# Where the moving operand lies against the weights: other offsets inside three buffers

## The chip, the core and the metric

The kernel runs on one core of a Trainium2 chip. The metric is the device time of one execution in microseconds (us), lower is better. Before the change three runs gave a median of 2787.92 us (2786.68 to 2790.01).

Names used below: PE is TensorE (matmuls), PEld its weight loads, DVE is VectorE, ACT ScalarE, POOL GpSimd, SP SyncE. SBUF is the on-chip memory of 128 partitions from which the engines read, PSUM the memory into which matmuls accumulate.

## The reference

Two layers of a decoder trunk on 256 tokens of width 2048, in float32. Each layer is a mixer, a gated feed-forward with a causal convolution, and an additive embedding:

```python
for layer in range(DEPTH):
    mix = mixer_hgrn2_gla(x, ...) if layer % 2 == 0 else mixer_rwkv7_gdn(x, ...)
    x = layer_norm(ALPHA * x + mix, ln_mix_w[layer], ln_mix_b[layer])
    x = layer_norm(ALPHA * x + conv_ffn(x, ffn_w_up[layer], ffn_conv[layer], ffn_w_down[layer]), ...)
    x = x + jax.nn.sigmoid(x @ ple_w_gate[layer]) * (p[layer] @ ple_w_proj[layer])

def conv_ffn(x, w_up, conv_w, w_down):
    u = causal_dwconv(x @ w_up, conv_w)
    gate, val = jnp.split(u, 2, axis=-1)
    return (jax.nn.silu(gate) * val) @ w_down
```

`w_up` is 2048 x 11264, `w_down` 5632 x 2048. Each mixer has a large input projection (2048 to some 7200 or 7700 columns), recurrences over the 256 tokens, and an output projection of 2048 x 2048. The time goes into these dense products.

## The kernel before

**Data.** The state is kept transposed, with features on the partitions: 16 blocks (k) of 128 features by 256 tokens. Every dense operand is kept as two float32r halves, high and low, so that a product is made of three: weight high x state high, weight high x state low, weight low x state high. float32r is a 4-byte type that the PE multiplies in one pass; `split` (L256) makes the two halves of the weights: ACT casts `wr` to `wh` (L260), DVE subtracts to get `wl` (L261). `hilo` does the same for the state.

**The buffers of the change.** `operand` (L217) makes the buffers of the state: `bufA` and `bufB` with 16 blocks each, and, inside the feed-forward, `ht` with 6 blocks for the part of the hidden layer that does not fit into `bufA`. One block takes `XS` = 576 words of 4 bytes in a partition, that is 2304 bytes or 9 x 256. In it, from word `AOFF`, `BOFF` or `HOFF` on, stand the high half (256 tokens and two columns for layer-norm weights, 258 words) and behind it the low half, so the low half starts 1032 bytes, or 8 modulo 256, after the high half.

**Where things lie.** In the program that is built, `bufA` and `bufB` begin at byte 8320 and 45184 of a partition, both 128 modulo 256; `ht`, `wh` and `wl` begin at 160 modulo 256 in every one of their buffers, and the 128 columns of one block of weights take 512 bytes. So all blocks of all weights start at 160 modulo 256. With the offsets of before the high halves start at 128 + 96 = 224 (`bufA`, `bufB`) and 160 + 64 = 224 (`ht`): 64 bytes after the weights, modulo 256. The low halves are 72 bytes after them. The tile `plt` of the embedding projection has no offset; it starts at 224 in both halves. The allocation is the same before and after.

**Loops.** All matmuls go through `mm` (L269, L270). Each has its own load of a 128 x 128 block of weights. `acc2` (L281) is the common form: for each k one matmul of weight high with both halves of the state at once, 512 columns, and one of weight low with the high half, 256 columns. `acc` (L272) uses three of 256 columns, for which `dense_raw` (before a layer norm has ended) adds the two columns, 258. `dense_tok` and `start_tok` give token-major results: there the state block is the stationary operand, and 512 columns of weights move. Feed-forward: up-projections read `bufB` (the first ten read `bufA`, 258 columns), down-projections read `bufA` and `ht`. The second mixer's input projection reads `bufA` in the form `acc`, with the recurrences' small matmuls between them, in an order that `drive` writes out.

**Order.** Each engine runs its program in order. SP issues the weights' DMAs three tiles ahead (`RB`), ACT and DVE split them into three buffers (`WB`), PE consumes them, and results leave PSUM through ACT and DVE.

Of the kernel before, what the change touches and what calls it, by code (L numbers as in the profile page):

```python
# [25 lines left out]
ALPHA = 4.0 ** 0.25  # L26
EDEC = math.exp(-0.5)
XS = 576
AOFF = 24
BOFF = 24  # L30
HOFF = 16
RS = 1024.0
KB = 4
SL = 2
# [162 lines left out]
class Trunk:  # L197
    def __init__(self, ctx, tc, a, out):
# [7 lines left out]
        c = self.const  # L206
        self.Ax = self.operand(c, KT, "bufA", AOFF)
        self.Bx = self.operand(c, KT, "bufB", BOFF)
        self.A, self.B = self.Ax[:, :, :, :S], self.Bx[:, :, :, :S]
# [531 lines left out]
    def ffn(self, l, X, Xx, U, Ux):  # L741
        up, dn = self.a[f"up{l}"], self.a[f"dn{l}"]
        Ht = self.operand(self.ev, 2 * DH - KT, "ht", HOFF)[:, :, :, :S]
        H = [U[:, j] if j < KT else Ht[:, j - KT] for j in range(2 * DH)]
# [677 lines left out]
```

## Time and profile before

| | before |
|---|---|
| median of three runs | 2787.92 us |
| profiled execution | 2788.15 us |
| its span, first to last instruction | 2786.4 us |
| PE busy | 2749.1 us, 99% |
| weight loads (beside PE) | 2488.9 us, 89% |
| DVE busy | 2068.9 us, 74% |
| ACT busy | 1606.1 us, 58% |
| DMA, bytes read from HBM | 478.32 MB |
| granted TensorE clock, mean | 0.997 |

The span is what lies between the first and the last instruction of the profiled execution; 1.75 us lie around it. A busy share counts a matmul from its start to its modelled end. Matmuls overlap in a pipeline (a 256-column matmul lasts some 280 ns by its record), so what a matmul costs is read from the distance between one start and the next. Weight loads have a row of their own, PEld, and run beside the matmuls.

### The profile page before, as it was taken

To read this page: it belongs to the slowest core of one execution; us is meant where nothing else is said; L and a number is where in the kernel's file an instruction comes from. 1 tells how busy PE (TensorE), PEld (TensorE's weight loads), DVE (VectorE), ACT (ScalarE), POOL (GpSimd) and SP (SyncE) were. 2 spreads that over 40 slices of the span, in tenths; PEclk is the share of its full clock that TensorE was granted. 3 is DMA by queue.
4 is the path that set the end of the run, shared out by engine and by line. 5 is a ranking of instruction groups with operands and counts; after the bars stand their busy time and mean duration, and the time that the engine had idled before them with its cause. 6 is when DMAs were issued, how large, how long until landed. Compare 5 with 4: busy or idle time off the path is not lost.

```text
span 2786.4 us, 48101 instructions
## 1 busy us (share of the span) xinstructions
PE 2749.1 (99%) x18433; PEld 2488.9 (89%) x18433; DVE 2068.9 (74%) x3899; ACT 1606.1 (58%) x2698; POOL 62.8 (2%) x99
## 2 busy tenths in 40 slices
PE   9999999999999999999999999999999999999999
PEld 7888889988888888899999899899988888888898
DVE  5775778877667776787579789778977666777787
ACT  5664556755445555556566676745855445555565
POOL 0000000000000000000011111000000000000000
PEclk9999999999999999999999999999999999999999
DMA  7555555666666666656444333345566666665665
GB/s 238 161 164 155 170 181 177 190 191 188 178 190 202 188 189 179 185 184 213 157 131 118 107 118 122 102 147 178 184 189 190 179 189 199 190 188 177 187 190 175
DMA packets 147943, 483.57 MB, mean 174 GB/s; under 512 B 16672, under 2 KB 19888, under 8 KB 147712
## 3 DMA queue, kind: packets, MB, share of 16 engines
q1 hardware_dynamic: 145968, 475.98, 56.6%
q0 software_dynamic: 1280, 3.94, 0.5%
q8 instruction: 145, 2.38, 0.4%
q14 instruction: 86, 0.70, 0.1%
q10 hardware_dynamic: 464, 0.57, 0.1%
HBM read 478.32 MB, written 2.11 MB: 172 GB/s over the span
## 4 chain that ended last, share of the span: by engine, by line
PE 91%; DVE 4%; ACT 3%; DMA 1%; issue 1%; SPq 0%; ACTq 0%; DVEq 0%
PE pd L270 76%; PE pm L270 14%; DVE wl L261 1%; ACT wh L260 1%; DMA wr<-pg 1%; ACT L350 0%; DMA wr<-ewv 0%; DVE z L353 0%; PE pm L541 0%; DVE rdo L353 0%; DVE gG L458 0%; ACT gE L350 0%; DMA wr<-owo 0%; ACT L1130 0%; ACT ron L350 0%
## 5 line engine op out<-in xcount | busy, mean ns | idle before, releaser
L261 DVE TENSOR_TENSOR wl<-wr,wh 128x1024 fp32r<-128x1024 f32 (+3 forms) x983 | 1112.7, 1132 | 433.4 <-ACT wh L260 430.0
L260 ACT CAST wh<-wr 128x1024 fp32r<-128x1024 f32 (+3 forms) x983 | 959.0, 976 | 701.0 <-PE pd L270 494.2
L270 PE MATMUL pd<-bufB,wh 128*128 128x512 f32 (+1 forms) x3264 | 1042.9, 376 | 0.9 <-DVE z L359 0.9
L270 PE MATMUL pd<-bufA,wh 128*128 128x256 f32 (+1 forms) x3744 | 1008.4, 341 | 1.3 <-ACT wh L260 1.3
L270 PE MATMUL pd<-bufB,wl 128*128 128x256 f32 x3008 | 815.5, 281 | 0.0
L270 PE MATMUL pd<-bufA,wl 128*128 128x256 f32 x2768 | 763.8, 283 | 1.4 <-DVE wl L261 1.2
L270 PEld LDWEIGHTS pd<-bufA,wh 128*128 128x128 f32 x3744 | 643.7, 191 | 69.7 <-ACT wh L260 1.6
L270 PEld LDWEIGHTS pd<-bufB,wh 128*128 128x128 f32 x3264 | 590.6, 190 | 104.0 <-ACT wh L260 1.1
L270 PEld LDWEIGHTS pd<-bufB,wl 128*128 128x128 f32 x3008 | 565.7, 188 | 13.3
L270 PEld LDWEIGHTS pd<-bufA,wl 128*128 128x128 f32 x2768 | 522.8, 189 | 12.2 <-DVE wl L261 3.3
L300 ACT COPY dsum<-pd 128x256 f32<-128x256 f32 x204 | 75.9, 372 | 254.5 <-PE pd L270 254.4
L353 DVE TENSOR_TENSOR dsum<-dsum,pd 128x256 f32<-128x256 f32 x204 | 85.8, 421 | 128.1 <-ACT dsum L300 127.9
L359 DVE SCALAR_TENSOR_TENSOR cu<-dsum,col,cu 128x255 f32<-128x255 f32 (+1 forms) x312 | 150.3, 482 | 5.6
L270 PE MATMUL pm<-bufB,wh 128*128 128x258 f32 x768 | 139.6, 284 | 1.5 <-DVE bufB L359 1.5
L270 PE MATMUL pd<-ht,wh 128*128 128x512 f32 x384 | 136.0, 392 | 0.0
L270 PEld LDWEIGHTS pm<-bufB,wh 128*128 128x128 f32 x768 | 118.4, 189 | 2.2 <-DVE bufB L359 1.9
L270 PE MATMUL pm<-bufA,wh 128*128 128x258 f32 x640 | 116.0, 284 | 0.0
L270 PE MATMUL pm<-bufB,wl 128*128 128x258 f32 x384 | 108.7, 283 | 0.8 <-DVE wl L261 0.8
L270 PE MATMUL pd<-ht,wl 128*128 128x256 f32 x384 | 107.3, 279 | 0.0
L270 PEld LDWEIGHTS pm<-bufA,wh 128*128 128x128 f32 x640 | 98.6, 189 | 0.3 <-DVE bufA L359 0.2
L270 PE MATMUL pm<-bufA,wl 128*128 128x258 f32 x320 | 90.3, 282 | 0.0
L270 PEld LDWEIGHTS pd<-ht,wh 128*128 128x128 f32 x384 | 73.1, 190 | 15.9
(366 smaller groups left out, 2648.0 us busy)
## 6 DMA issues: line engine op xcount, KB each, us to landing
wr<-up SPq DMA_DIRECT2D x352, 512.0 KB, 4.2
wr<-ow SPq DMA_DIRECT2D x120, 512.0 KB, 3.9
wr<-dn SPq DMA_DIRECT2D x128, 384.0 KB, 3.4
wr<-ew SPq DMA_DIRECT2D x82, 512.0 KB, 4.1
wr<-dn SPq DMA_DIRECT2D x128, 320.0 KB, 3.1
wr<-pg SPq DMA_DIRECT2D x64, 512.0 KB, 4.5
wr<-ewo SPq DMA_DIRECT2D x32, 512.0 KB, 4.4
wr<-ewv SPq DMA_DIRECT2D x30, 512.0 KB, 3.9
```

The lines of the kernel that those rows point to most:

```text
L260: self.nc.scalar.copy(wh, w)
L261: self.nc.vector.tensor_sub(wl, w, wh.bitcast(F32))
L270: return self.nc.tensor.matmul(o, lhsT=l, rhs=r, start=start, stop=stop)
L300: self.nc.scalar.copy(u, o[:, S:])
L353: self.nc.vector.tensor_tensor(o, a, b, op)
L359: self.nc.vector.scalar_tensor_tensor(o, a, s, b, op0, op1)
```

## The change

Three constants change, and with them where in its block of 2304 bytes the state stands: `bufA` from byte 96 to 48, `bufB` from 96 to 128, `ht` from 64 to 208. The high halves then start at 176, 0 and 112 modulo 256, which is 16, 96 and 208 bytes after the weights, and the low halves at 24, 104 and 216. In the token-major products, in which the weights move and `bufA` is stationary, the moving operand starts 240 (232 for the low half) bytes after the stationary one instead of 192 (184).

```diff
@@ -26,9 +26,9 @@
 ALPHA = 4.0 ** 0.25
 EDEC = math.exp(-0.5)
 XS = 576
-AOFF = 24
-BOFF = 24
-HOFF = 16
+AOFF = 12
+BOFF = 32
+HOFF = 52
 RS = 1024.0
 KB = 4
 SL = 2
```

Instructions, their order on each engine and all tile addresses are the same.

## Rows read from the trace of the kernel before

**Rows 1.** The page's part 1: busy time, share of the span, count of instructions.

```profile
PE 2749.1 (99%) x18433; PEld 2488.9 (89%) x18433; DVE 2068.9 (74%) x3899; ACT 1606.1 (58%) x2698; POOL 62.8 (2%) x99
```

**Rows 2.** The page's part 4: the chain that ended last, by engine.

```profile
PE 91%; DVE 4%; ACT 3%; DMA 1%; issue 1%; SPq 0%; ACTq 0%; DVEq 0%
```

**Rows 3.** PE's waits: waiting line, awaited line, us in total, times, longest.

```profile
PE pd L270 <- ACT wh L260: 7.6, 3, 5.8
```

**Rows 4.** The view of the cores: span, mean granted TensorE clock.

```profile
core 0: 2786.4 us, clock 0.997
```

**Rows 5.** Timeline, PE, dense stretch: start us, us, engine, line, operation, operands, count.

```profile
1050.32 0.40 PE L270 MATMUL pd<-bufB,wh 128*128 128x512 f32 x1
1050.55 0.28 PE L270 MATMUL pd<-bufB,wl 128*128 128x256 f32 x1
1050.67 0.39 PE L270 MATMUL pd<-bufB,wh 128*128 128x512 f32 x1
1050.90 0.28 PE L270 MATMUL pd<-bufB,wl 128*128 128x256 f32 x1
```

**Rows 6.** Timeline, weight loads (PEld) of the same stretch.

```profile
1050.55 0.19 PEld L270 LDWEIGHTS pd<-bufB,wh 128*128 128x128 f32 x1
1050.67 0.19 PEld L270 LDWEIGHTS pd<-bufB,wl 128*128 128x128 f32 x1
```

**Rows 7.** The chain in order of time: start us, us, engine and line, matmuls merged.

```profile
47.75 2.77 PE pd L270 x12
...
467.06 63.03 PE pm L270 x527
530.09 590.25 PE pd L270 x3390
...
1331.97 13.38 PE pm L270 x62
...
1398.52 2.94 PE pd L270 x24
```

**Rows 8.** Timeline, PE, the embedding projection (plt), first and tenth matmul.

```profile
518.63 0.40 PE L270 MATMUL pm<-plt,wh 128*128 128x256 f32 x2
...
519.68 0.28 PE L270 MATMUL pm<-plt,wh 128*128 128x256 f32 x1
```

**Rows 9.** The page's part 5: groups on line 270 (xcount | busy us, mean ns).

```profile
L270 PE MATMUL pd<-bufB,wh 128*128 128x512 f32 (+1 forms) x3264 | 1042.9, 376 | 0.9 <-DVE z L359 0.9
L270 PE MATMUL pd<-bufA,wh 128*128 128x256 f32 (+1 forms) x3744 | 1008.4, 341 | 1.3 <-ACT wh L260 1.3
L270 PE MATMUL pd<-bufB,wl 128*128 128x256 f32 x3008 | 815.5, 281 | 0.0
L270 PE MATMUL pd<-bufA,wl 128*128 128x256 f32 x2768 | 763.8, 283 | 1.4 <-DVE wl L261 1.2
...
L270 PE MATMUL pm<-bufB,wh 128*128 128x258 f32 x768 | 139.6, 284 | 1.5 <-DVE bufB L359 1.5
L270 PE MATMUL pd<-ht,wh 128*128 128x512 f32 x384 | 136.0, 392 | 0.0
...
L270 PE MATMUL pm<-bufA,wh 128*128 128x258 f32 x640 | 116.0, 284 | 0.0
L270 PE MATMUL pm<-bufB,wl 128*128 128x258 f32 x384 | 108.7, 283 | 0.8 <-DVE wl L261 0.8
L270 PE MATMUL pd<-ht,wl 128*128 128x256 f32 x384 | 107.3, 279 | 0.0
...
L270 PE MATMUL pm<-bufA,wl 128*128 128x258 f32 x320 | 90.3, 282 | 0.0
```

**Rows 10.** Timeline, PE, token-major products, every third matmul.

```profile
250.41 0.40 PE L270 MATMUL pd<-wl,bufA 128*128 128x512 f32 x1
...
251.11 0.39 PE L270 MATMUL pd<-wl,bufA 128*128 128x512 f32 x1
...
251.79 0.40 PE L270 MATMUL pd<-wl,bufA 128*128 128x512 f32 x1
```

## The prediction

> **What bounds the kernel now.** I read the busy shares first, then the chain of waits, then PE's own waits, the groups of instructions, and last the timeline of single matmuls. PE (TensorE) is busy 2749.1 of 2786.4 us, 99% of the span [rows 1]; 91% of the chain that ended last is PE, nearly all of it line 270, the one matmul helper [rows 2]. What PE waits for in total is small: its longest entry is 7.6 us for a weight split on ACT [rows 3]. The granted clock is 0.997 over the span, so nothing is to be had or lost there that the rows show [rows 4]. DVE, ACT and POOL have slack [rows 1]; the time is the number of matmuls times the distance from one start to the next. What a change of operand addresses can touch is that distance alone.
>
> **How far the starts are apart.** In the timeline of an undisturbed dense stretch, a 512-column matmul starts 0.23 us before the next one, a 256-column one 0.12 us [rows 5], and each weight load starts at the hundredth of a microsecond at which the matmul before it starts [rows 6]: the load of the next weights runs while the moving operand of the present matmul is read. That is the overlap in which the address distance could matter. More digits come from the chain, whose pieces merge many matmuls: 3390 in 590.25 us is 174.1 ns a matmul, or 348.2 ns for one pair of 512 and 256 columns; 527 matmuls (mostly 258 columns) in 63.03 us is 119.6 ns each; 24 matmuls of 256 columns in the second mixer take 2.94 us, 122.5 ns each [rows 7]. The projection of the per-layer embedding, whose moving tile starts 64 bytes after the weights in both halves, goes at (519.68 - 518.63) us over 9 matmuls, 116.7 ns [rows 8]. So 256 columns cost 116.7, 119.6 or 122.5 ns at distances of 64 and 72 bytes, depending on the place; the spread is 5.8 ns.
>
> How fast PE could go without any loss is bounded by plain fp32 matmuls: 62 of them in the decay LoRA take 13.38 us, 215.8 ns each [rows 7]. If such a record is two passes over 256 columns, a pass is 107.9 ns, with a full weight load under every record. Against this the dense pair loses 348.2 - 3 x 107.9 = 24.5 ns, 12 ns a matmul, and the 258-column stretch 11.7 ns. About 12 ns per dense matmul is therefore time that some arrangement of reads might win or double.
>
> **The change part by part.** No instruction is added, removed or moved; each engine's program has the same instructions in the same order, and no tile changes its address. Only where the operand lies inside its tile moves: bufA from 96 to 48 bytes, bufB from 96 to 128, ht from 64 to 208. The counts are in the groups of the page [rows 9]: bufA is the moving operand of 3744 + 2768 + 640 + 320 = 7472 matmuls, bufB of 3264 + 3008 + 768 + 384 = 7424, ht of 384 + 384 = 768; together 15664. In a few hundred more (the token-major products at the start and near 220 to 263 us) bufA is the stationary side and the weights move.
>
> The writes of these buffers by ACT and DVE shift too. I cost them at nothing: they run beside a PE that waits for them a few us in all [rows 3], and if one became slower, only the ends of a stage (layer norm, the last output) would show it, by less than a microsecond each.
>
> The cost per matmul isn't shown by before at the new distances, so it is bounded. From below: all of the 12 ns goes away, 15664 x 12 = 188 us, 2600 us. From above: it doubles, 2976 us. Between these the nearest rows say:
> - 8 bytes more costs little. In the 258-column stretch the second matmul of each k-step reads the low half, 72 bytes from the weights, the other two the high half at 64; in the embedding projection all three are at 64. The former takes 119.6 - 116.7 = 2.9 ns more a matmul, of which two more columns make 0.8 (107.9 / 256 each); 2.1 ns are left, at most.
> - Distances of 192 and 184 bytes occur in the token-major products, where the weights move and bufA is stationary: 12 matmuls of 512 columns take 2.77 us, 230.8 ns each [rows 7], against 0.23 us in the dense pair. That is up to 0.8 ns dearer, less than 1%. But there the spacing isn't even: the third matmul of each triple starts at 250.41, 251.11, 251.79, and so triples of 0.70 and 0.68 us alternate [rows 10]. Addresses alternate only in multiples of 512 bytes there, so a small shift in how the two reads meet changes a triple by some 10 to 20 ns. I take this as the sign that the reads do disturb each other and that the price depends on phase.
>
> From these I choose by buffer. **bufB, 96 bytes**: nearest to the 72 and 64 that it has now, which lie within 2.1 ns of each other with either sign open; no cost. **ht, 208 bytes**: nearest to 192; 0.8 ns x 768 = 0.6 us. **bufA, 16 bytes**: no row is near it, and it is the new distance closest to both reads beginning at the same place modulo 256. I take half of the spread that 256 columns show, 2.9 ns a matmul: 7472 x 2.9 = 21.7 us. The token-major products go from 192 to 240 bytes, 16 short of a full turn; the same 2.9 ns on their 384 [rows 9] is 1.1 us. Sum: 0.6 + 21.7 + 1.1 = 23.4 us. All of it is on the path, since PE is the path; nothing hides it. The profiled execution took 2788.15 us, 1.75 more than its span and 0.2 more than the median of the three runs (2787.92), so 2788.15 + 23.4 = 2811.5, say 2811 us.
>
> A rule speaks against the whole mechanism. The Trainium skill (SBUF — State Buffer, "Who interferes with whom") gives PE two read ports, one for the moving operand and one for weight loads, independent of each other, and names only the port pair of VectorE and GpSimd as a place of contention. By that the sum is zero. The trace neither proves nor refutes it: every dense matmul in it overlaps with a load. A second page pulls the other way: the Trainium skill (TensorE: Matmul & The Clock Gate, "Back-to-back issue gap") has an isolated warm matmul at its columns over 2.4 GHz plus 2.5 ns, by which the 512-column one would take 215.8 ns and the 256-column one 109.2; the rows show 230 and 117 to 122. This page differs from the trace by 7 to 14 ns, so something that it leaves out costs time here.
>
> **The rivals.**
> 1. *The two reads don't interact.* The 12 ns belong to this data type's streaming or to the switch of weights, whatever the addresses. For it: 184, 192, 64 and 72 bytes come within 1 ns on average. Against it: the uneven triples. Time: 2788.
> 2. *The new distances are better.* If bufB's 96 bytes lets the load pass without a clash and saves a quarter of the 12 ns, with bufA and ht as before, 7424 x 3 = 22 us go: 2766. For it: the excess at 64 bytes is large, so 64 is no distance without loss. Against it: 72 isn't better than 64. This is the case that ends on the other side; it decides as soon as the saving on bufB exceeds the loss on bufA, since the two have the same number of matmuls.
> 3. *Head-on reads.* At 16 bytes the load and the stream of bufA start nearly on the same spot and the excess on bufA doubles: 7472 x 12 = 90 us, 2878. For it: nothing in before is that near. Against it: a load covers 512 bytes and a 256-column stream 1024 in the same 0.12 us, so the two can't stay at one distance; they sweep through all of them whatever the start.
>
> **How the numbers follow.** Forecast (a few ns on bufA, 2795 to 2845) 0.45; rival 1 0.21; rival 2 0.19; rival 3 or something near it on bufB 0.15. What a measurement of this kernel can tell from no change is about 0.2%, 5.6 us. Faster 0.19, the same 0.21, slower 0.45 + 0.15 = 0.60. The range reaches down to rival 2's time and up to a large part of rival 3's: 2766 to 2866.
>
> **What would show it.** In the changed kernel's trace, the start-to-start distance of matmuls by moving buffer: bufA's pairs some 6 ns longer than 348, bufB's unchanged, ht's within 2 ns. The up-projections (bufB) and the down-projections (bufA with ht) of one layer stand side by side in the 590 us stretch, so its length should grow by less than bufA's share; PE's count of instructions, its waits and the granted clock should be as before. The prediction is wrong if bufA and bufB change by the same amount, if bufB changes more, or if neither moves by a nanosecond.

## The result, and the profile after

The changed kernel takes 2808.15 us (median of four runs, 2805.95 to 2813.13) against 2788.97 us of the kernel before in the same runs: a ratio of 1.0069, 95% interval 1.0053 to 1.0085. It is slower, by 19 us. The forecast was 2811 us.

PE is still the bound. Part 1 of the changed kernel's page and its view of the cores, against [rows 1, 4]:

```profile
PE 2768.1 (99%) x18433; PEld 2484.8 (89%) x18433; DVE 2071.6 (74%) x3899; ACT 1605.2 (57%) x2698; POOL 63.7 (2%) x99
```

```profile
core 0: 2804.2 us, clock 0.998
```

PE's busy time grew by 19.0 us (2768.1 - 2749.1), and the span by 17.8 us (2804.2 - 2786.4), at the same instructions and, within 0.001, the same granted clock. Its longest wait in total, of the view of PE's waits, is as small as in [rows 3]:

```profile
PE pd L270 <- ACT wh L260: 6.9, 2, 5.5
```

So the time went into the distance from matmul to matmul. The chain in order of time, with the pieces that answer to [rows 7]:

```profile
47.73 2.80 PE pd L270 x12
...
470.20 63.98 PE pm L270 x527
534.17 597.64 PE pd L270 x3390
...
1343.40 13.38 PE pm L270 x62
...
1409.28 2.89 PE pd L270 x24
...
2015.46 597.64 PE pd L270 x3390
```

The feed-forward's stretch of 3390 matmuls grew from 590.25 to 597.64 us, and it occurs once in each layer. The second one of the kernel before, which [rows 7] don't show, is as long as the first:

```profile
2006.76 590.25 PE pd L270 x3390
```

So 2 x 7.4 = 14.8 of the 17.8 us stand in these two rows. The token-major products went from 230.8 to 233.3 ns a matmul (2.80 / 12), the 258-column stretch from 119.6 to 121.4 (63.98 / 527). The plain fp32 matmuls, which read none of the three buffers, are unchanged at 13.38 us for 62, and the second mixer's 256-column ones became cheaper, 120.4 ns (2.89 / 24) for 122.5.

Which buffer and which width is it? In a dense stretch of `bufB`, to be held against [rows 5], the timeline shows:

```profile
1054.95 0.40 PE L270 MATMUL pd<-bufB,wh 128*128 128x512 f32 x1
1055.19 0.28 PE L270 MATMUL pd<-bufB,wl 128*128 128x256 f32 x1
1055.31 0.40 PE L270 MATMUL pd<-bufB,wh 128*128 128x512 f32 x1
1055.54 0.28 PE L270 MATMUL pd<-bufB,wl 128*128 128x256 f32 x1
```

A pair now takes 0.36 us (1054.95 to 1055.31) where it took 0.35, and the 512-column matmul is what grew. The timeline rounds to 0.01 us. For the rest of this document I use the start times of all matmuls in the trace, matched instruction by instruction between two traces (the programs are the same), and take the distance from each start to the next, by the moving buffer. "Steady" means leave out distances over 280 ns (512 columns) or 160 ns (fewer), which hold a wait. Summed over everything the changes make 18.1 us, against 17.8 us of the span:

| moving operand | columns | count | steady mean, before -> after, ns | change in all, us |
|---|---|---|---|---|
| bufB (96 bytes) | 512 | 2752 | 230.69 -> 236.35 | +15.5 |
| bufB | 256 | 3520 | 117.87 -> 117.10 | -2.8 |
| bufB | 258 | 1152 | 120.05 -> 120.04 | 0.0 |
| bufA (16 bytes) | 512 | 1792 | 230.61 -> 233.03 | +4.0 |
| bufA | 256 | 4745 | 118.37 -> 117.98 | -2.7 |
| bufA | 258 | 960 | 120.03 -> 122.19 | +2.0 |
| ht (208 bytes) | 512 | 384 | 230.00 -> 234.90 | +1.9 |
| ht | 256 | 384 | 116.67 -> 117.66 | +0.4 |
| weights (token-major) | 512 | 384 | 231.30 -> 233.35 | +0.7 |
| all others | | 2359 | | -0.9 |

By buffer that is bufB 12.7, bufA 3.3, ht 2.3 and the token-major products 0.7 us. The total came out as forecast, and its places did not: the forecast had 21.7 us on bufA and nothing on bufB.

### The profile page after: what moved, and what is told of

It reads as the page before. It is cut to its first block, busy times and chain, and to the rows that moved or that the text cites. A ratio compares the mean times of both kernels' runs of the same rounds, so it can differ in the third digit from the quotient of the medians.

```text
span 2804.2 us, 48101 instructions
## 1 busy us (share of the span) xinstructions
PE 2768.1 (99%) x18433; PEld 2484.8 (89%) x18433; DVE 2071.6 (74%) x3899; ACT 1605.2 (57%) x2698; POOL 63.7 (2%) x99
## 4 chain that ended last, share of the span: by engine, by line
PE 91%; DVE 4%; ACT 3%; DMA 1%; issue 1%; SPq 0%; ACTq 0%; DVEq 0%
PE pd L270 76%; PE pm L270 14%; DVE wl L261 1%; ACT wh L260 1%; DMA wr<-pg 1%; ACT L350 0%; DMA wr<-ewv 0%; DVE z L353 0%; DMA out<-ply 0%; PE pm L541 0%; DVE gG L458 0%; DVE s L353 0%; ACT gE L350 0%; ACT L1130 0%; DVE rdo L353 0%
## 5 line engine op out<-in xcount | busy, mean ns | idle before, releaser
L270 PE MATMUL pd<-bufB,wh 128*128 128x512 f32 (+1 forms) x3264 | 1054.0, 379 | 0.8 <-DVE z L359 0.8
L270 PEld LDWEIGHTS pd<-bufB,wh 128*128 128x128 f32 x3264 | 582.7, 187 | 117.8 <-issue 0.9
L270 PEld LDWEIGHTS pd<-bufB,wl 128*128 128x128 f32 x3008 | 564.6, 188 | 15.5
L270 PEld LDWEIGHTS pd<-bufA,wl 128*128 128x128 f32 x2768 | 522.7, 189 | 12.7 <-DVE wl L261 3.1
L270 PEld LDWEIGHTS pm<-bufB,wh 128*128 128x128 f32 x768 | 118.4, 188 | 2.2 <-DVE bufB L359 1.7
L270 PE MATMUL pm<-bufA,wh 128*128 128x258 f32 x640 | 118.0, 288 | 0.0
L270 PE MATMUL pd<-ht,wl 128*128 128x256 f32 x384 | 107.9, 281 | 0.0
```

The lines of the kernel that those rows point to most:

```text
L270: return self.nc.tensor.matmul(o, lhsT=l, rhs=r, start=start, stop=stop)
```

## The experiments

Each ratio is against runs of the kernel before on the same chip, with its 95% interval.

**One buffer at a time.** Theory: each buffer has its own price, set by its distance, and the prices add. Rival: the forecast's own account, in which bufA carries the loss.

```diff
-AOFF = 24
+AOFF = 12
```

> bufA alone is moved to 16 bytes from the weights; bufB and ht stay at 64. By the prediction's account (bufA carries the loss, 2.9 ns on each of its 7472 matmuls): 2811 us, +0.8%. By the account read from the changed kernel's trace (the loss is bufB's 512-column matmuls, bufA adds 4 us in its 512-column ones, 2 in its 258-column ones and gives 3 back in its 256-column ones, the token-major products add 1): about 2792 us, +0.15%.

Measured: 2792.16 us, ratio 1.0013 (1.0004 to 1.0022).

```diff
-BOFF = 24
+BOFF = 32
```

> bufB alone is moved to 96 bytes; bufA and ht stay at 64. By the prediction's account (96 bytes cost nothing): 2788 us. By the account read from the changed kernel's trace (512-column matmuls of bufB 5.7 ns longer, its 256-column ones 0.8 ns shorter): +13 us, 2801 us, +0.45%.

Measured: 2802.11 us, ratio 1.0049 (1.0035 to 1.0062). The chain's pieces, first with bufA alone moved, then with bufB alone:

```profile
471.46 63.53 PE pm L270 x527
534.99 590.61 PE pd L270 x3390
```

```profile
468.42 63.02 PE pm L270 x527
531.44 595.55 PE pd L270 x3390
```

The 258-column stretch, which reads bufA, moves with bufA alone (63.53 us for 63.03), the long stretch with bufB (595.55 for 590.25) and hardly with bufA (590.61). The ratios add: 0.13% + 0.49% = 0.62%, and 2.3 us of ht's are 0.08%, against 0.69%. The forecast's account falls.

These two runs also show what a mean of single matmuls is worth. `ht` stayed at 64 bytes in both, and yet its 512-column matmuls went from 230.0 to 228.4 and 227.9 ns, its 256-column ones from 116.7 to 118.5 and 118.8. The sum of the two, one pair, stayed at 346.7 to 346.9 ns. Time can move from one matmul to its neighbour, so below the pair stands beside the single means. A pair is the steady distance from a 512-column matmul to a 256-column one of the same buffer, plus that from a 256-column one to a 512-column one; before, bufB and bufA both have 348.2 ns.

**Distance, or the buffer's own alignment?** With bufB at 96 bytes its high half starts at 0 modulo 256, with bufA at 16 bytes at 176. It could be this address itself that costs, with no part in it of the weights. So everything is moved together: the weights' buffers, and all behind them, 32 bytes on by an unused tile, the state 32 bytes on in its blocks.

```diff
-AOFF = 24
-BOFF = 24
+AOFF = 32
+BOFF = 32
...
-        self.mk = {}
+        self.mk = {}; self.pad = c.tile([P, 8], F32, name="pad")
```

> An unused tile of 32 bytes moves the weights' buffers and everything behind them on by 32 bytes, and AOFF and BOFF go to 32, so that bufA, bufB and ht all start at 0 modulo 256, where bufB starts in the changed kernel, with all distances to the weights at 64 as before. Theory 1 (the distance between the two reads decides): as before, 2788 us, pairs of 512 and 256 columns at 230.7 and 118 ns. Theory 2 (the alignment of the moving operand's own address decides): the 512-column matmuls of bufA, bufB and ht go to 236 to 237 ns as bufB's do in the changed kernel, 256-column ones to 117; 4928 x 5.7 - 8265 x 0.8 = +21 us, 2810 us.

Measured: 2789.54 us, ratio 1.0005 (0.9996 to 1.0014). The chain's pieces:

```profile
470.15 63.03 PE pm L270 x527
533.17 590.25 PE pd L270 x3390
```

63.03 and 590.25 us, to the hundredth what [rows 7] show. bufB's 512-column matmuls take 230.67 ns (before 230.69), although they start where they started in the changed kernel. Theory 2 falls: what counts is the distance between the state and the weights.

**The curve.** Four more runs put other distances into the three buffers. Theory 1a: modulo 64, so that multiples of 64 are alike. Rival 1b: modulo 256, worst where both reads begin at one place.

```diff
-AOFF = 24
-BOFF = 24
-HOFF = 16
+AOFF = 40
+BOFF = 8
+HOFF = 48
```

> Distances 128 (bufA), 0 (bufB) and 192 (ht), all multiples of 64 as the 64 of before is, at the same weights. Theory 1a (distance modulo 64): as before, 2788 us, 230.7 and 118 ns in all three buffers. Theory 1b (distance modulo 256, worst where both reads begin at one place): bufB at 0 slower than the 236.4 ns that it has at 96, so over +14 us, 2802 us or more; bufA and ht anywhere between 230 and 237 ns.

Measured: 2805.2 us, ratio 1.0061 (1.0048 to 1.0074). The time is as 1b expected, but bufB's 512-column matmuls take 234.0 ns: more than 1a's 230.7, less than the 236.4 that 1b wanted to see exceeded.

```diff
-AOFF = 24
-BOFF = 24
-HOFF = 16
+AOFF = 16
+BOFF = 48
+HOFF = 32
```

> Distances 32 (bufA), 160 (bufB) and 128 (ht), to fill the curve of price against distance. If the price goes by distance modulo 64: 32 and 160 cost what 96 costs, 236 ns for 512 columns, about 353 ns for a pair against 348.6, about 2812 us. If it goes modulo 256 only, 32 lies between 16 (233 ns) and 64 (230.7), 160 is open between 230 and 237, and ht at 128 shows the 229.2 ns that bufA has there.

Measured: 2804.58 us, ratio 1.0054 (1.0038 to 1.007). bufA at 32 bytes is cheaper than at 16 and at 64, and ht at 128 has 231.0 ns for the 229.2 expected.

```diff
-AOFF = 24
-BOFF = 24
-HOFF = 16
+AOFF = 56
+BOFF = 20
+HOFF = 8
```

> Distances 192 (bufA), 48 (bufB) and 32 (ht). If the price goes by the distance alone: bufA at 192 shows the 233 ns that ht has there, ht at 32 shows what bufA has at 32 in the run before, and bufB at 48 lies between 230.7 and 234 ns; 2785 to 2800 us.

Measured: 2796.31 us, ratio 1.0021 (1.0011 to 1.0032), as expected.

```diff
-AOFF = 24
-BOFF = 24
-HOFF = 16
+AOFF = 0
+BOFF = 40
+HOFF = 20
```

> Distances 224 (bufA), 128 (bufB) and 80 (ht), to fill the curve. bufB at 128 should show the 229.2 ns (512 columns) and 119 to 121 (256, 258) that bufA has there; ht at 80 lies between 230 (64) and 236 (96); bufA at 224 between 233 (192, 208) and 234 (0). 2788 to 2796 us.

Measured: 2801.88 us, ratio 1.0042 (1.0028 to 1.0056). The time is above what was expected. The trace's span is 10.9 us longer than before, of which 9 are bufA's: its 256-column matmuls went from 118.4 to 120.1 ns at 224 bytes, more than at any other distance of bufA.

The long stretch in the chain shows bufB's distance at a glance, since 2495 of its 3390 matmuls read bufB. In this order, one fence each: bufB at 0 (with bufA at 128), at 160 (32), at 48 (192) and at 128 (224):

```profile
532.47 596.72 PE pd L270 x3390
```

```profile
530.90 595.96 PE pd L270 x3390
```

```profile
533.11 591.97 PE pd L270 x3390
```

```profile
533.14 591.42 PE pd L270 x3390
```

**The same distances, the other way round.** Is it the distance, or what bufB and bufA are used for?

```diff
-AOFF = 24
-BOFF = 24
-HOFF = 16
+AOFF = 32
+BOFF = 12
+HOFF = 0
```

> The distances of the changed kernel with bufA and bufB swapped (96 and 16), and 0 for ht. If the price belongs to the distance: bufA's 512-column matmuls take 236 to 237 ns, bufB's 233 and ht's 234 ns; 1792 x 5.8 + 2752 x 2.5 = +17 us, less about 3 for the 256-column ones, 2803 us. If it belongs to the buffer (what reads bufB, or where it lies): bufB's stay at 236, bufA's at 233, and the time at 2808 us.

Measured: 2809.13 us, ratio 1.0069 (1.0049 to 1.0089); the long stretch:

```profile
535.29 595.82 PE pd L270 x3390
```

bufB at 16 bytes has 232.8 ns for 512 columns (bufA had 233.0 there) and 122.2 ns for 258 (bufA 122.2); bufA at 96 has 234.0 (bufB 236.4). But bufA's 256-column matmuls gave nothing back where bufB's had become cheaper: a pair at 96 bytes takes 353.1 ns in bufA and 352.9 in bufB. At 16 bytes it takes 351.0 in bufB and 351.2 in bufA. So at these two distances the price of a pair goes with the distance, not with the buffer. The time, 2809 instead of the 2803 expected, is over by terms that the expectation had wrong or left out: the 256-column matmuls cost 2.7 us where about 3 were to come back, ht 2.1, the token-major products 1.5 and bufB's 258-column matmuls 1.2; the 512-column ones of bufA and bufB cost 5 us less than it said.

All distances, steady means in ns of 512- and 256-column matmuls and, behind the semicolon, of a pair (bufA's 256-column ones are in part those of the form `acc`, which the pair leaves out):

| distance, bytes | bufB | bufA | ht |
|---|---|---|---|
| 0 | 234.0, 119.3; 353.3 | | 234.0, 118.2; 352.1 |
| 16 | 232.8, 118.1; 351.0 | 233.0, 118.0; 351.2 | |
| 32 | | 228.9, 118.4; 347.7 | 228.2, 119.0; 347.4 |
| 48 | 232.4, 116.7; 348.4 | | |
| 64 (before) | 230.7, 117.9; 348.2 | 230.6, 118.4; 348.2 | 230.0, 116.7; 346.7 |
| 80 | | | 234.0, 118.4; 352.7 |
| 96 | 236.4, 117.1; 352.9 | 234.0, 118.9; 353.1 | |
| 128 | 228.8, 118.6; 347.7 | 229.2, 118.2; 347.7 | 231.0, 117.2; 348.0 |
| 160 | 234.7, 118.6; 352.9 | | |
| 192 | | 233.3, 118.5; 352.1 | 233.1, 118.2; 351.5 |
| 208 | | | 234.9, 117.7; 352.9 |
| 224 | | 232.2, 120.1; 352.9 | |

Neither 1a (0, 64, 128 and 192 differ by some 5 ns) nor a simple hump around 0 holds. By the pairs there are two levels: 346.7 to 348.4 ns at 32, 48, 64 and 128 bytes, and 351.5 to 353.3 at 0, 80, 96, 160 and 192 to 224, with 16 a little below the upper one at 351. Single means scatter more than that: 32 and 48 differ by 4 ns in 512 columns and by 1 in a pair. There is no smooth curve to read a value from: 64 and 80 bytes lie on different levels, and so do 128 and 160.

That the period is 256 bytes was taken for granted, and the traces leave it open. Successive blocks of the state lie 2304 bytes apart, those of the weights 512, so the distance modulo 512 alternates from block to block. At 0, 64 and 96 bytes bufB's 512-column matmuls don't alternate after the first blocks of a product; at 128 they do, between 225 and 232 ns, and at 160 between 238 and 232.

**Which load is it?** Each matmul has two blocks of weights near it: its own, already loaded, and the next, which is being loaded. They started at the same place modulo 256 so far. Moving `wl` alone tells them apart.

```diff
-HOFF = 16
+HOFF = 24
...
-        wl = self.ring.tile([P, 1024], F32R, name="wl", tag="wl", bufs=WB)[:, :m]
+        self.gap = getattr(self, "gap", None) or self.ring.tile([P, 56], F32, name="gap", tag="gap", bufs=1); wl = self.ring.tile([P, 1024], F32R, name="wl", tag="wl", bufs=WB)[:, :m]
```

> Only the low halves of the weights (wl) are moved on by 224 bytes, to 128 modulo 256, by an unused tile between wh and wl; the high halves wh and the state stay, so the state lies 64 bytes from wh and 96 from wl. In the common form the 512-column matmul (weights wh) runs while wl is loaded, and the 256-column one (weights wl) while the next wh is loaded. Theory N (what meets the stream is the load of the next weights): the 512-column matmuls of all three buffers go to 236 to 237 ns, as bufB's do at 96 bytes, and the 256-column ones stay near 118; 4928 x 5.8 = +29 us, 2817 us. Theory O (the address of the weights that the matmul itself uses): 512 columns stay at 230.7 ns, 256 columns lose about 1 ns; 2788 us or a little less.

Measured: 2806.81 us, ratio 1.0064 (1.0047 to 1.008). The timeline of a dense stretch of bufB, and the long stretch in the chain:

```profile
1052.81 0.40 PE L270 MATMUL pd<-bufB,wh 128*128 128x512 f32 x1
1053.05 0.28 PE L270 MATMUL pd<-bufB,wl 128*128 128x256 f32 x1
1053.16 0.40 PE L270 MATMUL pd<-bufB,wh 128*128 128x512 f32 x1
1053.40 0.28 PE L270 MATMUL pd<-bufB,wl 128*128 128x256 f32 x1
```

```profile
533.29 596.28 PE pd L270 x3390
```

The 512-column matmuls use `wh`, which did not move, and they grew as at 96 bytes: 235.6 ns in bufB, 235.7 in bufA, 235.6 in ht. The 256-column ones use the `wl` that moved, and did not grow (116.6, 117.4, 116.7). The pairs of bufB and bufA, 352.1 and 352.0 ns, are nearly those at 96 bytes from both halves (352.9). So it is the load of the next weights, running beside the stream, that sets the price, and nearly all of it arises beside the 512-column matmul; theory O falls. That the new place of `wl` costs by itself isn't excluded by this run, but with bufB alone at 96 bytes `wl` stayed where it was, and bufB's pair takes the same 352.9 ns. The time stayed under the 2817 us expected, since the 256-column matmuls became about 1 ns cheaper, as they had in the changed kernel.

**Where in the load?** If the two reads disturb each other all along, a shorter load must cost less.

```diff
-            self.mm(o[:, :S], wl, x[:, 0], False, False)
+            self.mm(o[:32, :S], wl[:, :32], x[:, 0], False, False)
```

> As before, but in the common form (acc2) the product of the weights' low half uses the first 32 of 128 columns alone, so that the weight load that runs beside the 512-column matmul reads 128 bytes in place of 512; three quarters of the low-half product is left out, and the result is not the reference's. The distance stays 64. If the 17 ns that a 512-column matmul takes over its 213.3 ns of columns come from the load beside it: the matmul falls from 230.7 to 215 to 220 ns, 4928 x 12 = 59 us less, about 2730 us. If they belong to the stream of this data type: 230 ns as before, 2788 us; then the distance decides only over what comes on top.

Measured: 2785.97 us, ratio 0.9986 (0.9976 to 0.9996). The weight loads by form are indeed shorter, 110 ns by their records where [rows 6] show 0.19 us:

```profile
L270 PEld LDWEIGHTS pd<-bufB,wl 128*32 128x32 f32 x2752 | 302.6, 110 | 27.4
L270 PEld LDWEIGHTS pd<-bufA,wl 128*32 128x32 f32 x1792 | 195.6, 109 | 20.7 <-DVE wl L261 3.1
```

```profile
530.47 586.95 PE pd L270 x3390
```

But the matmul beside them isn't: bufB's 512-column ones take 232.0 ns, not 215 to 220, and the next 256-column ones 114.4. The expectation missed; the kernel gained 0.14%, not the 2% that 2730 us would have been. The same edit on the changed kernel:

> The changed kernel (16, 96 and 208 bytes) with the shortened low-half load of the run before: 32 of 128 columns, three quarters of the low-half product left out. At the old distance the short load left the 512-column matmuls at 232 ns. If the 5.7 ns that 96 bytes add to bufB's 512-column matmuls arise along the load's 512 bytes, as the two reads drift past each other: they fall to 232 to 233 ns, as at 64, and the time is that of the short load at 64, about 2786 us. If they arise in the load's first 128 bytes or where both reads begin: 236 to 238 ns remain, +0.5%, about 2800 us.

Measured: 2787.64 us, ratio 0.9996 (0.9986 to 1.0005) to the kernel before.

```profile
533.72 589.78 PE pd L270 x3390
```

Here the 512-column matmuls of bufB fall from 236.3 to 228.2 ns. The pair of bufB (start distances of all neighbours, some 2580 of each kind in each trace) tells it best, here with no distance left out:

| low-half load | at 64 bytes | at 96 bytes |
|---|---|---|
| 128 columns | 230.7 + 117.6 = 348.3 | 236.3 + 116.7 = 353.0 |
| 32 columns | 232.0 + 114.4 = 346.4 | 228.2 + 119.2 = 347.4 |

With the full load 96 bytes cost 4.7 ns a pair, with a quarter of it 1.0. Most of the price of the distance thus depends on the rest of the load, behind its first 128 bytes. The state stands and is written where it does in the changed kernel, so its place and its writes alone don't make the price. At the short load 346.4 ns are left, against 323.7 for three passes of 107.9 (if, as the prediction assumed, a plain fp32 matmul of [rows 7] is two such passes). Leaving out three quarters of the low half's load took only 1.9 ns off the pair. One reservation: the shortened matmul also fills only 32 columns of the array, and the load of `wh` beside the 256-column matmul stayed whole.

**A better pair of distances.** The table has 32 bytes as cheap as 64 or cheaper.

```diff
-AOFF = 24
-BOFF = 24
+AOFF = 16
+BOFF = 16
```

> bufA and bufB at 32 bytes from the weights, ht at 64. If the price goes by the distance alone, bufB's 512-column matmuls go from 230.7 to 228.9 ns, as bufA's did at 32, with 256- and 258-column ones unchanged: 2752 x 1.8 = 5 us less on bufB and 3 us on bufA, of which a part was seen to turn into waits: 2782 to 2787 us, -0.1% to -0.25%. If bufA's value at 32 was owed to something else in its stages: 2789 us.

Measured: 2785.58 us, ratio 0.9987 (0.9979 to 0.9996).

```profile
467.88 63.02 PE pm L270 x527
530.90 588.66 PE pd L270 x3390
```

bufB's 512-column matmuls take 228.8 ns, the long stretch 588.66 us. This kernel is faster than both others, than the one before by 0.13%: bufB's 512-column matmuls give 5.1 us, of which its 256-column ones take back 3.2. On bufA the steady 512-column matmuls got 1.9 ns cheaper, 3.4 us, but only 0.5 us of it reached the sum over all distances; the rest is in longer distances that hold waits. By pairs, bufB and bufA went from 348.2 to 347.5 and 347.6 ns. `ht`, which stayed at 64 bytes, went from 346.7 to 349.7, 1.0 us in all: so a buffer's pair doesn't follow its own distance alone, and what moved `ht`'s is open.

## Why the prediction was right or wrong

- **What bounds the kernel.** Right: PE, by the distance between starts. Instructions, waits and clock stayed, and the loss is in those distances.
- **The reads disturb each other by distance.** Right, and shown: one distance with all addresses moved costs nothing (1.0005), the same address of bufB with another distance costs 0.49%; moving `wl` alone puts it on the load of the next weights, and shortening that load takes most of the price away (4.7 to 1.0 ns a pair). Why some distances cost and others don't, no run shows.
- **bufB at 96 bytes costs nothing.** This is the step that failed. It rested on 96 being near 72 and 64, as if the price were a smooth function of distance. It is not: 5.7 ns on 2752 matmuls of 512 columns, 15.5 us, less 2.8 on the 256-column ones, so 12.7 us in place of nothing. And a start at 72 bytes was seen only where the low half streams by itself, in matmuls of 256 and 258 columns, which at 96 bytes changed by -0.8 and 0.0 ns; no row showed a 512-column matmul of the state at any distance but 64.
- **bufA at 16 bytes costs 2.9 ns a matmul, 21.7 us.** Missized: 3.3 us. The 2.9 ns were half of a spread of 256-column matmuls between places of the program at nearly one distance, so it held no price of a distance; at 16 bytes those matmuls changed by -0.4 ns. The spread was also read too wide: its lower end, 116.7 ns, comes from two starts that are rounded to 0.01 us, and all 192 distances of that projection have a mean of 117.7. The 512-column matmuls (+2.4) and the 258-column ones (+2.2) did change. That two wrong terms made nearly the right sum is a coincidence.
- **ht at 208 bytes, 0.6 us; token-major products, 1.1 us.** Measured 2.3 and 0.7 us. The neighbour at 192 was the wrong row for ht, because there the weights stream and the state is loaded; ht itself has 233.1 ns at 192. (The 384 token-major products are not among [rows 9], but the count is right.)
- **The uneven triples as a sign of phase.** Borne out as far as the price does depend on how two streams meet; that the unevenness itself has this cause was not tested.
- **Rival 1, no interaction.** It falls. By the Trainium skill (SBUF — State Buffer, "Who interferes with whom") PE's two read ports are independent; here the time of a matmul depends on where the weights that are being loaded lie, by up to 7.6 ns in 229 (bufB at 128 and at 96 bytes), and that of a pair by 5.2. The measurement decides.
- **Rival 2, bufB better at 96.** It falls, but its reason holds: 64 was not without loss, since 32 is 0.13% better.
- **Rival 3, head-on reads.** Only a start: a pair of bufA at 16 bytes takes 3.0 ns more than at 64, one of bufB at 0 bytes 5.1 more, not 12 more a matmul, and 80 and 96 bytes cost as much as 0. The argument against it, that the two reads sweep past each other from any start, fits these small prices, but it took the load to last the 0.12 us of a 256-column matmul; by its record it lasts 0.19 us [rows 6].
- **What would show it wrong.** "If bufB changes more" was named as the sign of a wrong prediction, and it is what happened.

## What to carry to other kernels

Where weight loads run beside streaming matmuls, the distance modulo 256 between the moving operand and the weights that load at that moment is worth one scan: it moved this kernel between 0.9987 and 1.0069 of its time at no cost in instructions. Scan it and read each buffer's start-to-start distance from the trace, by pairs of neighbouring matmuls; don't interpolate, since distances 16 or 32 bytes apart differed nearly as much as any two (bufB's pair at 128 and 160 bytes 347.7 and 352.9 ns, ht's at 64 and 80 bytes 346.7 and 352.7). One run can carry one distance per buffer, and shifting everything together shows whether distance or address is at work.

## What the runs showed of the hardware that was not expected

- Loading a quarter of the weights' columns beside a 512-column matmul (110 for 188 ns by the load's record) did not shorten that matmul at 64 bytes: 232.0 for 230.7 ns. What makes most of its 15 ns over two passes of 107.9 (with the prediction's assumption on a pass) stays open.
- Time moves between neighbours: a distance that makes the 512-column matmul dearer often makes the 256-column one after it cheaper (bufB at 96 bytes +5.7 and -0.8 ns; at 128 bytes -1.9 and +0.7). The sum of a pair says better what a distance costs: on it, buffers at one distance agree within some 1.5 ns, while their 512-column means differ by up to 2.4.
- In bufB the price is repeatable to the ns: in the changed kernel 2148 of bufB's 2752 distances of 512 columns were 237 or 238 ns, and with all addresses moved by 32 bytes the stretch of 3390 matmuls came back to the same 590.25 us. Not all is so firm: with bufA alone moved, the embedding projection, of which nothing had moved, went from 117.7 to 115.6 ns a matmul, and `ht`'s pair at 64 bytes lay at 346.7 or at 349.7 ns.
